# Three stages of a two-layer hybrid block trade places: hyena beside the second recurrent phase, attention after it, output weights where hyena was

## Chip, cores and metric

One core of one Trainium2 chip. The metric is device time in microseconds (us) of one execution; lower is better. The engines are named as in the profile: PE (TensorE matmul), PEld (its weight load), DVE (VectorE), ACT (ScalarE), POOL (GpSimd), SP (SyncE, which issues most of the transfers).

## The reference, cut to what matters

Two layers. In each, a normalised stream goes through one input projection, four mixers work on their parts of it, and an output projection adds the gated result to the stream. 1024 latent tokens, 256 context tokens, width 1024; each mixer has width 256.

```python
h_l = rms_norm(x, norm_g) * (1.0 + scale[:, None]) + shift[:, None]
hy_l, hyg_l, rw_l, rwg_l, wa_l, wag_l, fa_l, fag_l = jnp.split(h_l @ w_in, SPLIT_IDX, axis=-1)
a_l = hyena_branch(hy_l, ...) * jax.nn.silu(hyg_l)       # long convolution by FFT
b_l, b_c = rwkv_mixer(rw_c, rw_l, ...)                   # recurrent, both directions
c_l = window_attention(...) * jax.nn.silu(wag_l)         # +-128 tokens, and the context
d_l = dense_attention(...) * jax.nn.silu(fag_l)          # all 1280 tokens
mix_l = jnp.concatenate([a_l, b_l, c_l, d_l], axis=-1)
x = x + gate[:, None] * (mix_l @ w_out)
```

The context tokens pass through the same weights in the first layer and are not put out by the second. `scale`, `shift` and `gate` come from a modulation, silu(c) times a 1024 x 3072 matrix for each layer.

## The kernel before

The program is one straight stream of instructions, traced stage by stage (`program`, from L1573). A scheduler orders the instructions of each engine ahead of time, by the order in which they are traced and by a timing model of its own; at run time each engine, and each transfer queue, works its list in order. A tile waits by semaphores for earlier users of its addresses.

Tiles come from pools. A pool lies on the left or on the right side of SBUF: left pools are stacked upwards from 18.6 KB (per partition), right pools downwards from 224 KB; a closed pool's place is free for later pools of its side, and pools of opposite sides may overlap when they are open at different times. In both layers of the kernel before the stages lie as follows.

- Left: the projection's operands `hhi`, `hlo` (18.6 to 98.6 KB), above them the projection's own pool `pj` (to 137.7, with two buffers each of `wr`, `wh`, `wl`), above it the attention projection's pool `pa` (137.7 to 203.5). When operands and projection are done, attention's pool `at` takes 18.6 to 98.
- Right: hyena's filters first; in layer 0 then two modulations `mod` (209.8 to 224, three buffers of `mw`), one for the gate of this layer and one for the next layer; then phase A of the recurrence with its constants (204 to 224) and work tiles (138 to 204); then phase B (138.5 to 224); then hyena (102 to 224; `F` at 102 to 110); after it the output projection's weights and work tiles (99.9 to 224).

The stages: `Proj.rw` projects the seven recurrent blocks, with a convolution. `Proj.attn` (L295) projects queries, keys and values. `Rwkv.phase_a` (L444) prepares ten blocks of 128 tokens and after the 4th, 8th and 10th runs `solve`, 31 short steps on DVE and POOL. `Rwkv.phase_b` (L659) takes the ten blocks from both ends: `stage_b` loads `IN`, `yc`, `nn`, multiplies small blocks on PE, and `chain` carries the state; blocks that come too early for one direction are stored in `st_d` and taken up by `pend` at the end, seven of them after the tenth block. `hyena` (L1360) transforms, multiplies with `Kf` (two buffers) and transforms back, mostly on DVE and POOL. `attention` (L919) runs for a = 0, the windowed part, and a = 1, the dense part, in blocks of 128 queries: scores (L981), softmax, transposes, values; `om` at L1028 ends a block. `OutProj` (L1070) loads and splits the output weights (`wor`), then `tiles` works 128 tokens at a time; in the first layer it also writes the next layer's `hhi`, `hlo`, over attention's pool, and holds an `xt` tile (two buffers) until then.

The projection's other 14 blocks (three gates, six hyena blocks, one more gate) are `Proj.beside` (L283). Two of them go early (`PACE['pre']`); the rest is traced after phase B and is filler. It is paced by marks: each block of phase A sets a mark of weight 1.3, each of phase B one of 1.0 (the first 4.5), each of the last seven `pend` calls 0.5, 30 in all. A piece of projection may not be queued on PE ahead of the mark that its share falls to, between the fractions `f0` and `f1` of all marks.

Of the kernel before, what the change touches and what calls it, by code (L numbers as in the profile page):

```python
# [12 lines left out]
PSUM = bass.MemoryType.PSUM  # L13
# [10 lines left out]
PACE = {'pre': (2, 2), 'w0': (0.0, 0.0), 'wt': (3.5, 3.5), 'f0': (0.3, 0.3), 'f1': (0.7, 0.7)}  # L24
# [1335 lines left out]
def hyena(k, l, kd, sp, pp):  # L1360
# [27 lines left out]
    def forward(o_, hf):  # L1388
        u = U[hf]
        Kf = tile_([R, 2, 128], "Kf", 2, p)  # L1390
# [179 lines left out]
_OUT = (L, D)  # L1570


def program(nc, tc, A, out):  # L1573
# [3 lines left out]
    R = "right"  # L1577
    with k.pool("cp", 1) as cp, k.pool("dp", 1, DRAM) as dp:
        setup(k, cp, dp)

        def filters(l):
            for nm, f, _, shape in hyenas[:2 if l < DEPTH - 1 else 1]:
                k.kd[l, nm] = dp.tile(shape, F32, name=f"kd{l}{nm}")
                with tc.using_default_side(R), k.pool(f"hf{l}{nm}") as sp, k.pool(f"hfp{l}{nm}", 1, PSUM) as pp:
                    run(f(k, l, k.kd[l, nm], sp, pp))

        k.kd = {}
        for l in range(DEPTH):
            last = l == DEPTH - 1
            rw = Rwkv(k, l, cp, dp)  # L1590
            with ExitStack() as es:
                if l == 0:
                    held = ExitStack()
                    with tc.using_default_side(R):
                        ap = es.enter_context(k.pool("raw"))
                    hi, lo = norm_in(k, held.enter_context(k.pool(f"hp{l}")), ap)
                filters(l)
            with held:
                with k.pool(f"pj{l}") as sp, k.pool(f"pjp{l}", 1, PSUM) as pp:
                    w = Proj(k, l, hi, lo, sp, pp)  # L1600
                    run(w.rw())
                    todo = [(g, i) for g in (1, 2, 3, "h", 0) for i in range(6 if g == "h" else 2)]
                    early = PACE["pre"][l]
                    w.beside(todo[:early])
                    if not last:
                        for a, parts in ((l, (1,)), (l + 1, (0, 1))):
                            with tc.using_default_side(R), k.pool(f"mod{a}") as rs, k.pool(f"modp{a}", 1, PSUM) as rp:
# [3 lines left out]
                    with tc.using_default_side(R), k.pool(f"re{l}") as re, k.pool(f"ra{l}") as rs, k.pool(f"rap{l}", 1, PSUM) as rp:  # L1611
                        run(rw.phase_a(re, rs, rp))
                    with tc.using_default_side(R), k.pool(f"rb{l}") as rs, k.pool(f"rbp{l}", 1, PSUM) as rp:
                        run(rw.phase_b(rs, rp))
                    w.beside(todo[early:], PACE["f0"][l], PACE["f1"][l])
# [45 lines left out]
```

## Time and profile before

| | |
|---|---|
| median of 3 runs | 2611.66 us (2608.37 to 2614.43) |
| the profiled execution, its own time | 2599.59 us |
| span from its first to its last instruction | 2597.8 us |
| PE busy | 2294.4 us (88%) |
| DVE / ACT / POOL busy | 1696.6 / 1105.8 / 1012.8 us |
| mean granted TensorE clock | 0.913 of full |

Busy time is the time in which an engine had an instruction running; PE's is longer where the clock is at its lower level. The stages of layer 0, in us from the span's start: projection and filters to 264, attention projection and modulation to 434, phase A with its last solve to 722, phase B to 1040 (its seven late `pend` calls from 965), attention from 866 to 1278, hyena within that from 1040 to 1250, output projection to 1410. Layer 1: attention projection to 1719, phase A to 2010, phase B to 2292, hyena 2293 to 2461, attention 2119 to 2510, output projection to 2592.

### The profile page before, as it was taken

To read this page: it belongs to the slowest core of one execution; us is meant where nothing else is said; L and a number is where in the kernel's file an instruction comes from. 1 tells how busy PE (TensorE), PEld (TensorE's weight loads), DVE (VectorE), ACT (ScalarE), POOL (GpSimd) and SP (SyncE) were. 2 spreads that over 40 slices of the span, in tenths; PEclk is the share of its full clock that TensorE was granted. 3 is DMA by queue.
4 is the path that set the end of the run, shared out by engine and by line. 5 is a ranking of instruction groups with operands and counts; after the bars stand their busy time and mean duration, and the time that the engine had idled before them with its cause. 6 is when DMAs were issued, how large, how long until landed. Compare 5 with 4: busy or idle time off the path is not lost. (4 is left out here: it accounts for less than half of the span.)

```text
span 2597.8 us, 45285 instructions
## 1 busy us (share of the span) xinstructions
PE 2294.4 (88%) x16864; PEld 1873.1 (72%) x16864; DVE 1696.6 (65%) x3669; ACT 1105.8 (43%) x2622; POOL 1012.8 (39%) x1279
## 2 busy tenths in 40 slices
PE   7799999889999898878897997998999979887698
PEld 3688678667788786656686887976777868666466
DVE  6985247698734567797344776677886345779933
ACT  5422224444232576545444221344443347654451
POOL 1631223366622114464322233324676211336542
PEclk9899998779999899889998998987799989998799
DMA  7223773544364746411444124335445475641152
GB/s 261 93 90 112 247 219 116 151 143 147 107 228 141 196 150 159 165 33 70 139 129 133 72 74 152 114 112 147 136 133 161 161 201 171 163 154 49 42 162 98
DMA packets 288696, 359.12 MB, mean 138 GB/s; under 512 B 108007, under 2 KB 229910, under 8 KB 283100
## 3 DMA queue, kind: packets, MB, share of 16 engines
q1 hardware_dynamic: 264008, 271.04, 33.6%
q0 software_dynamic: 11232, 70.78, 7.9%
q10 hardware_dynamic: 13236, 14.40, 2.0%
q8 instruction: 133, 2.18, 0.3%
q14 instruction: 87, 0.71, 0.1%
HBM read 227.31 MB, written 128.84 MB: 137 GB/s over the span
## 5 line engine op out<-in xcount | busy, mean ns | idle before, releaser
L232 POOL TENSOR_TENSOR wl<-wr,wh 128x1024 fp32r<-128x1024 f32 x58 | 145.1, 2507 | 276.2 <-ACT wh L231 198.9
L986 DVE TENSOR_REDUCE st<-S 128x1 f32<-128x512 f32 (+1 forms) x320 | 173.2, 557 | 102.0 <-PE S L982 57.7
L245 PE MATMUL acc<-hhi,wh 128*128 128x512 f32 (+1 forms) x896 | 222.8, 387 | 15.0 <-ACT wh L231 10.0
L981 PE MATMUL S<-kp,qs 128*128 128x256 f32 (+2 forms) x384 | 151.0, 402 | 85.5 <-ACT P L996 64.1
L245 PE MATMUL acc<-hlo,wh 128*128 128x512 f32 (+1 forms) x896 | 215.8, 376 | 2.6 <-DVE hlo L211 2.6
L996 ACT ACTIVATE P<-S,st 128x512 f32<-128x512 f32 (+1 forms) x320 | 184.2, 588 | 79.4 <-DVE st L989 74.2
L245 PE MATMUL acc<-hhi,wl 128*128 128x512 f32 (+1 forms) x896 | 216.0, 376 | 0.0
L245 PEld LDWEIGHTS acc<-hhi,wh 128*128 128x128 f32 x896 | 160.8, 198 | 50.4 <-ACT wh L231 11.9
L1012 PE MATMUL pt<-ident,P 128*128 128x128 f32 x976 | 169.0, 296 | 29.8 <-ACT PT L952 23.3
L245 PEld LDWEIGHTS acc<-hlo,wh 128*128 128x128 f32 x896 | 157.8, 193 | 33.5 <-DVE hlo L211 3.1
L952 ACT COPY PT<-pt 128x512 f32<-128x512 f32 (+2 forms) x298 | 141.0, 497 | 88.0 <-PE pt L1012 86.2
L245 PEld LDWEIGHTS acc<-hhi,wl 128*128 128x128 f32 x896 | 155.1, 191 | 31.7 <-issue 3.2
L1012 PEld LDWEIGHTS pt<-ident,P 128*128 128x128 f32 x976 | 122.1, 150 | 61.6 <-ACT PT L952 30.7
L981 PEld LDWEIGHTS S<-kp,qs 128*128 128x128 f32 x384 | 78.5, 205 | 114.9 <-ACT P L996 78.0
L1022 PE MATMUL O<-PT,V 128*64 128x256 f32 x976 | 132.1, 388 | 3.3 <-ACT PT L952 2.7
L982 PE MATMUL S<-kp,qs 128*128 128x256 f32 (+2 forms) x384 | 126.7, 342 | 3.7 <-DMA kp<-qk_d 3.7
L1022 PEld LDWEIGHTS O<-PT,V 128*64 128x64 f32 x976 | 70.6, 138 | 45.6 <-issue 6.7
L340 ACT ACTIVATE qx<-acc 128x256 f32<-128x256 f32 x76 | 29.2, 385 | 171.6 <-PE acc L335 152.5
L231 ACT ACTIVATE wh<-wr 128x1024 fp32r<-128x1024 f32 x58 | 60.7, 1057 | 94.3 <-PE acc L245 75.0
L589 PEld LDWEIGHTS p_g<-AR,BKT 64*128 64x128 f32 x640 | 77.0, 221 | 30.9 <-issue 6.8
L335 PE MATMUL acc<-wh,hhi 128*128 128x256 f32 x608 | 95.0, 298 | 4.5 <-ACT qx L340 2.5
L335 PE MATMUL acc<-wl,hhi 128*128 128x256 f32 x608 | 92.4, 290 | 6.4 <-POOL wl L232 6.4
(404 smaller groups left out, 5918.7 us busy)
## 6 DMA issues: line engine op xcount, KB each, us to landing
IN<-in_d POOLq DMA_DIRECT2D x18, 2048.0 KB, 9.4
wr<-in_w_in POOLq DMA_DIRECT2D x58, 512.0 KB, 4.6
mw<-in_mod_w SPq DMA_DIRECT2D x48, 512.0 KB
in_d<-BK SPq DMA_DIRECT2D x20, 512.0 KB
in_d<-AL SPq DMA_DIRECT2D x20, 512.0 KB
kp<-qk_d SPq DMA_DIRECT2D x32, 320.0 KB
qk_d<-qo SPq DMA_DIRECT2D x72, 128.0 KB
in_d<-GG SPq DMA_DIRECT2D x18, 512.0 KB
```

The lines of the kernel that those rows point to most:

```text
L231: w.k.nc.scalar.activation(h, r, AF.Copy)
L232: w.k.nc.gpsimd.tensor_tensor(lw, r, h.bitcast(F32), op=ALU.subtract)
L245: nc.tensor.matmul(ps[:, :n], a[:, kc * 128:(kc + 1) * 128], b[:, kc, t0:t0 + n], start=(i == 0 and kc == 0), stop=(i == 2 and kc == 7))
L335: nc.tensor.matmul(ps[:, :256], x_[:, kc, t * 128:(t + 1) * 128], w_[:, kc, :], start=(n == 0 and kc == 0), stop=(n == 2 and kc == 7))
L589: nc.tensor.matmul(pg[:, hp, c], BKT[q, hp, c], AR[q, :, hp, half(c)], start=True, stop=True)
L952: nc.any.tensor_copy(o, i)
L981: nc.tensor.matmul(ps[:, w0:w0 + w], qs[:, hd % 2, hd // 2], kp[kv][0][:, t0:t0 + w], start=True, stop=False)
L982: nc.tensor.matmul(ps[:, w0:w0 + w], qs[:, hd % 2, hd // 2], kp[kv][1][:, t0:t0 + w], start=False, stop=not masks)
L986: TR(ng[:, i:i + 1], ps[:, :w0], axis=AX.X, op=ALU.max, negate=True)
L996: nc.scalar.activation(P[:, :w], ps[:, :w], AF.Exp, bias=gm, accum_out=den[:, i:i + 1])
L1012: nc.tensor.transpose(pt[:, i, :], P[:, i * 128:(i + 1) * 128], k.ident)
L1022: nc.tensor.matmul(O[kv * 64:kv * 64 + 64, 0], V[:, t, kv * 64:kv * 64 + 64], PTs[kv][:, i], start=(i == 0), stop=(i == nt - 1))
```

## The change

The side of every pool is given by `near` and `far` of the layer: near is left in layer 0 and right in layer 1, far is the other. Operands, projection, hyena and output weights lie near; filters, modulations, the attention projection, phases A and B, then attention, lie far. Hyena's `Kf` has one buffer instead of two, so that its pool has 114 KB and in layer 0 lies at 18.6 to 132.6 KB, clear of phase B. In layer 0 the attention projection's pool then lies at 158 to 224 KB, attention's at 144 to 224 and the output projection's at 18.6 to 142.6; layer 1 is the mirror image. The second half of `program` keeps its order of tracing. `PACE` releases the projection's pieces from the fraction 0.0 to 0.5 of the marks instead of 0.3 to 0.7.

```diff
-PACE = {'pre': (2, 2), 'w0': (0.0, 0.0), 'wt': (3.5, 3.5), 'f0': (0.3, 0.3), 'f1': (0.7, 0.7)}
+PACE = {'pre': (2, 2), 'w0': (0.0, 0.0), 'wt': (3.5, 3.5), 'f0': (0.0, 0.0), 'f1': (0.5, 0.5)}
...
-        Kf = tile_([R, 2, 128], "Kf", 2, p)
+        Kf = tile_([R, 2, 128], "Kf", 1, p)
...
+SIDES = ("left", "right")
...
+            near, far = SIDES[l % 2], SIDES[1 - l % 2]
+            on = tc.using_default_side
...
-                filters(l)
-            with held:
-                with k.pool(f"pj{l}") as sp, k.pool(f"pjp{l}", 1, PSUM) as pp:
...
+                filters(l, far)
+            with held, on(near), k.pool(f"pj{l}") as sp, k.pool(f"pjp{l}", 1, PSUM) as pp:
...
+                with on(far):
                     if not last:
                         for a, parts in ((l, (1,)), (l + 1, (0, 1))):
-                            with tc.using_default_side(R), k.pool(f"mod{a}") as rs, k.pool(f"modp{a}", 1, PSUM) as rp:
+                            with k.pool(f"mod{a}") as rs, k.pool(f"modp{a}", 1, PSUM) as rp:
                                 modulation(k, a, parts, 3, rs, rp)
                     with k.pool(f"pa{l}") as sa, k.pool(f"pap{l}", 1, PSUM) as pq:
                         run(w.attn(sa, pq))
-                    with tc.using_default_side(R), k.pool(f"re{l}") as re, k.pool(f"ra{l}") as rs, k.pool(f"rap{l}", 1, PSUM) as rp:
+                    with k.pool(f"re{l}") as re, k.pool(f"ra{l}") as rs, k.pool(f"rap{l}", 1, PSUM) as rp:
                         run(rw.phase_a(re, rs, rp))
...
             with ExitStack() as es:
+                with on(near):
+                    for nm, _, f, _ in hyenas[:1 if last else 2]:
+                        with k.pool(f"hy{l}{nm}") as rs, k.pool(f"hyp{l}{nm}", 1, PSUM) as rp:
+                            run(f(k, l, k.kd[l, nm], rs, rp))
                 at = ExitStack()
-                for nm, _, f, _ in hyenas[:1 if last else 2]:
-                    with tc.using_default_side(R), k.pool(f"hy{l}{nm}") as rs, k.pool(f"hyp{l}{nm}", 1, PSUM) as rp:
-                        run(f(k, l, k.kd[l, nm], rs, rp))
-                sp, pp = at.enter_context(k.pool(f"at{l}")), at.enter_context(k.pool(f"atp{l}", 1, PSUM))
-                with tc.using_default_side(R):
+                with on(far):
+                    sp, pp = at.enter_context(k.pool(f"at{l}")), at.enter_context(k.pool(f"atp{l}", 1, PSUM))
+                with on(near):
                     op = OutProj(k, l, es.enter_context(k.pool(f"op{l}")), es.enter_context(k.pool(f"opp{l}", 1, PSUM)))
...
-                    hi, lo = operands(held.enter_context(k.pool(f"hp{l + 1}")))
...
+                    with on(far):
+                        hi, lo = operands(held.enter_context(k.pool(f"hp{l + 1}")))
```

## Rows read from the trace of the kernel before

**Rows 1.** The page: engine busy (share) xinstructions; a costliest group (busy, mean ns).
```profile
PE 2294.4 (88%) x16864; PEld 1873.1 (72%) x16864; DVE 1696.6 (65%) x3669; ACT 1105.8 (43%) x2622; POOL 1012.8 (39%) x1279
...
L986 DVE TENSOR_REDUCE st<-S 128x1 f32<-128x512 f32 (+1 forms) x320 | 173.2, 557 | 102.0 <-PE S L982 57.7
```

**Rows 2.** Busy time by stretch, layer 0; columns in the first line.
```profile
core 0: us, PE busy (x) PEld busy (x) DVE busy (x) ACT busy (x) POOL busy (x), PEclk, DMA share, GB/s
264.60:366.50 101.90, 99.49 (x654) 68.86 (x655) 27.57 (x123) 21.98 (x50) 19.16 (x13) 0.98 0.74 242
434.00:722.00 288.00, 258.83 (x1596) 206.94 (x1593) 225.57 (x425) 122.45 (x243) 159.40 (x280) 0.84 0.48 144
722.00:965.00 243.00, 227.85 (x2794) 199.78 (x2795) 117.36 (x355) 112.95 (x325) 51.12 (x93) 0.96 0.56 176
965.00:1040.00 75.00, 65.09 (x651) 48.41 (x650) 59.81 (x239) 52.55 (x170) 28.33 (x37) 0.95 0.57 147
1052.00:1215.00 163.00, 123.64 (x798) 99.21 (x798) 144.90 (x227) 79.50 (x215) 95.57 (x71) 0.85 0.21 71
1278.00:1410.00 132.00, 117.94 (x542) 97.42 (x542) 50.73 (x69) 59.64 (x130) 39.47 (x40) 0.93 0.35 113
```

**Rows 3.** The same view of layer 1: phase B, its end, the output projection.
```profile
2010.00:2219.00 209.00, 189.90 (x2429) 167.01 (x2429) 98.54 (x304) 107.06 (x314) 36.66 (x69) 0.96 0.57 179
2219.00:2292.00 73.00, 62.77 (x643) 44.96 (x640) 56.31 (x211) 49.08 (x146) 26.81 (x35) 1.00 0.49 131
...
2510.00:2592.00 82.00, 76.50 (x338) 63.01 (x336) 34.63 (x39) 15.58 (x22) 26.20 (x25) 0.98 0.33 112
```

**Rows 4.** Timeline of SP: start us, us, engine line op; phase B's last store, hyena.
```profile
1039.75 0.36 SPq L848 DMA_DIRECT2D mix_d<-om  x1
1040.41 0.35 SPq L1368 DMA_DIRECT2D F<-in_fw  x1
```

**Rows 5.** Timeline of all engines: the modulation's last store, phase A's first constant.
```profile
366.50 0.32 SPq L140 DMA_DIRECT2D mrow<-mr  x1
...
368.34 0.33 ACTq L456 DMA_DIRECT2D tri<-in_tri  x1
```

**Rows 6.** The modulation's loads, one line: ns min/median/max, first to last start.
```profile
L126 SPq DMA_DIRECT2D mw<-in_mod_w x29: 328/345/904, 265.7 to 358.0; - x29
```

**Rows 7.** Busy time of the modulation's matmuls (L129): PE, PEld, PEclk, DMA, GB/s.
```profile
264.60:366.50 101.90, 32.19 (x128) 3.35 (x128) 0.98 0.74 242
```

**Rows 8.** The same for the projection pieces' matmuls (L245) in phase B.
```profile
722.00:838.00 116.00, 73.20 (x345) 56.68 (x345) 1.00 0.49 166
```

**Rows 9.** One line: phase A's block stores; phase B's first matmuls, layers 0 and 1.
```profile
L621 SPq DMA_DIRECT2D in_d<-AL x10: 332/394/472, 459.4 to 671.7; - x10
...
L733 PE MATMUL p_t<-IN,Y x160: 270/275/484, 722.3 to 951.2; 128*128 128x128 f32 x160
...
L733 PE MATMUL p_t<-IN,Y x160: 270/275/553, 2009.6 to 2205.8; 128*128 128x128 f32 x160
```

**Rows 10.** Key tile `kp` in 700 to 900 us: first scores, key loads.
```profile
L981 PEld LDWEIGHTS S<-kp,qs x24: 186/190/331, 866.4 to 898.5; 128*128 128x128 f32 x24
...
L933 SPq DMA_DIRECT2D kp<-qk_d x8: 444/594/1663, 836.6 to 843.6; - x8
```

**Rows 11.** Timeline of POOL, layer 1: ends of two windowed, two dense blocks.
```profile
2245.00 0.73 POOL L1028 TENSOR_TENSOR om<-om,gt 128x256 f32<-128x256 f32 x1 [0.80 <-ACT om L1027]
2256.12 0.73 POOL L1028 TENSOR_TENSOR om<-om,gt 128x256 f32<-128x256 f32 x1
2283.13 0.74 POOL L1028 TENSOR_TENSOR om<-om,gt 128x256 f32<-128x256 f32 x1 [4.07 <-ACT om L1027]
2303.70 0.73 POOL L1028 TENSOR_TENSOR om<-om,gt 128x256 f32<-128x256 f32 x1 [12.77 <-ACT om L1027]
```

**Rows 12.** Line L1234 in hyena of layer 1: ns min/median/max.
```profile
L1234 DVE TENSOR_TENSOR W<-G x4: 1104/1534/2185, 2323.8 to 2434.8; 128x512 f32<-128x512 f32 x4
L1234 DVE TENSOR_TENSOR Z<-G x4: 675/886/1095, 2351.7 to 2453.5; 128x512 f32<-128x512 f32 x4
```

**Rows 13.** SP's waits, 2295 to 2462 us: waited for, us in total, times, longest.
```profile
SPq L1451 <- DVE zc L1447: 54.1, 1, 54.1
```

More of the change, by code (lines that the diff above doesn't have):

```diff
@@ L1576, in program, with filters @@
     run = lambda g: [None for _ in g]
-    R = "right"
     with k.pool("cp", 1) as cp, k.pool("dp", 1, DRAM) as dp:
         setup(k, cp, dp)
-        def filters(l):
+        def filters(l, side):
             for nm, f, _, shape in hyenas[:2 if l < DEPTH - 1 else 1]:
                 k.kd[l, nm] = dp.tile(shape, F32, name=f"kd{l}{nm}")
-                with tc.using_default_side(R), k.pool(f"hf{l}{nm}") as sp, k.pool(f"hfp{l}{nm}", 1, PSUM) as pp:
+                with tc.using_default_side(side), k.pool(f"hf{l}{nm}") as sp, k.pool(f"hfp{l}{nm}", 1, PSUM) as pp:
                     run(f(k, l, k.kd[l, nm], sp, pp))
@@ L1589, in program @@
             last = l == DEPTH - 1
+            near, far = SIDES[l % 2], SIDES[1 - l % 2]
+            on = tc.using_default_side
             rw = Rwkv(k, l, cp, dp)
-            with ExitStack() as es:
+            with ExitStack() as es, on(far):
                 if l == 0:
                     held = ExitStack()
-                    with tc.using_default_side(R):
-                        ap = es.enter_context(k.pool("raw"))
-                    hi, lo = norm_in(k, held.enter_context(k.pool(f"hp{l}")), ap)
-                filters(l)
-            with held:
-                with k.pool(f"pj{l}") as sp, k.pool(f"pjp{l}", 1, PSUM) as pp:
[L1600 to L1604, printed above, removed]
+                    ap = es.enter_context(k.pool("raw"))
+                    with on(near):
+                        hp = held.enter_context(k.pool(f"hp{l}"))
+                        hi, lo = norm_in(k, hp, ap)
+                filters(l, far)
+            with held, on(near), k.pool(f"pj{l}") as sp, k.pool(f"pjp{l}", 1, PSUM) as pp:
+                w = Proj(k, l, hi, lo, sp, pp)
+                run(w.rw())
+                todo = [(g, i) for g in (1, 2, 3, "h", 0) for i in range(6 if g == "h" else 2)]
+                early = PACE["pre"][l]
+                w.beside(todo[:early])
+                with on(far):
                     if not last:
                         for a, parts in ((l, (1,)), (l + 1, (0, 1))):
-                            with tc.using_default_side(R), k.pool(f"mod{a}") as rs, k.pool(f"modp{a}", 1, PSUM) as rp:
+                            with k.pool(f"mod{a}") as rs, k.pool(f"modp{a}", 1, PSUM) as rp:
                                 modulation(k, a, parts, 3, rs, rp)
@@ L1631, in program @@
                     held = ExitStack()
-                    hi, lo = operands(held.enter_context(k.pool(f"hp{l + 1}")))
-                    with k.pool(f"nrmp{l}", 1, PSUM) as pp:
-                        op.tiles([8, 9] + list(range(8)), out, (hi, lo, pp))
+                    with on(far):
+                        hi, lo = operands(held.enter_context(k.pool(f"hp{l + 1}")))
+                        with k.pool(f"nrmp{l}", 1, PSUM) as pp:
+                            op.tiles([8, 9] + list(range(8)), out, (hi, lo, pp))
 def arrays_of(inputs):
```

6 lines of the change are left out of this document (3 added, 3 removed).

## The prediction

> **What bounds the kernel now.** I read the page's engine line first, then the busy time by stage, then the gates between stages. TensorE (PE) is busy for 2294.4 of 2597.8 us [rows 1], so the time can only fall where PE idles or is granted its lower clock level. The stage views [rows 2, 3] show where that is. Phase A of the recurrence has a mean clock of 0.84, which is a mix of the two levels. Phase B is well filled in both layers (0.96), by projection pieces first and by attention later. The worst stretch is hyena beside attention: PE is busy for 123.6 of 163 us at clock 0.85, while VectorE (DVE) is busy for 144.9. So attention with phase B is a good pairing, attention with hyena a bad one, and phase A lacks filler in its first half. The change moves all three. I follow the time at which phase B starts, phase B's length, what is left after it, and the last projection.
>
> **Gates.** The sum hangs on one reading of the kernel: when a pool is placed on addresses of an older pool, its first instructions are queued behind the last of the older one. In this kernel hyena's first table F lies at 102 to 110 KB and phase B's pool only begins at 138.5 KB, but hyena's pool as a whole covers both. F is loaded right behind phase B's last store, at 1040.41 after 1039.75 [rows 4]. Likewise phase A's constant `tri`, at 206 KB, comes behind the modulation's last store, at 368.34 after 366.50 [rows 5], though the modulation lies above 209 KB. So I ask, for each pool, whom it overlaps after the change.
>
> **Part by part, first layer.** Phase B's start moves as follows.
> (1) The attention projection's pool goes to the far side, top-aligned at 158 to 224 KB. It now lies over the two modulations, which hold their place until their last load is used. Today both run together from 264.6 to 366.5. The modulation's 29 loads of 0.524 MB are 15.2 MB, 63 us at the 242 GB/s of that stretch [rows 2, 6]; I take 52, since alone they don't share the DMA engines. Its own matmuls keep PE busy for 32.2 us [rows 7]. Today modulation and attention projection end together at 434, 169 us after 264.6; then it would be 52 + (169 - 32) = 189, so +20 (0 if they still overlap, +31 at 63 us). Filler for that gap is unlikely: the loads of the attention projection's own weights take both `wr` buffers and wait.
> (2) Phase A's constants lie under the same pool and can't come early any more. From hyena's first load (1040.41) to the stretch that starts with its first transposes (1052) are 12 us [rows 2, 4]; the first pieces of the later projections have no mark to wait for and cover some: +8 (0 to 12).
> (3) The projection pieces. Marks weigh 13 for phase A, 13.5 for phase B's blocks, 3.5 for its end, 30 in all. Pieces were released between marks 9 and 21, now between 0 and 15, so 87% by the end of phase A's blocks. 73.2 us of them ran after 722 [rows 8] and move ahead. Phase A with its solves has 288 - 258.8 = 29 us of idle PE, and 16% of 288 = 46 us lost to the clock [rows 2], 75 in all, so they just fit: +6 (0 to 25). The last solve stays: between phase A's last block (671.7) and phase B's first matmul (722.3) are 51 us [rows 9]. Projection covers it today; then it is the pieces that are left and hyena's start, and what idles there costs no more than the 51 us already on the path.
> Together phase B starts 34 us later.
> (4) Phase B with hyena. B's ten blocks and its end take 722 to 1040, 318 us, and in layer 1 2010 to 2292, 282 us [rows 2, 3]; block starts are (951.2 - 722.3)/9 = 25.4 us apart in layer 0 and 21.8 in layer 1 [rows 9], with PE full. With hyena PE has room, but DVE hasn't: phase B's stretches hold 117 + 60 us and hyena's 145, less attention's share, of which the reductions alone are 173.2/2 = 87 a layer [rows 1, 2]. That leaves at most 235 us of DVE work. Taken at 19 us a block, 48 for the end (75 and 73 today with attention in it) and 22 for waits on SP (below), I get 260 and 256: -58 and -26. Lower end 225, at about the DVE work; upper end 300.
> (5) Attention now lies on the phase's side, 144 to 224 KB, and starts only at phase B's end. From its first key load to its first score matmul are 866.4 - 836.6 = 30 us today [rows 10], beside phase B's own loads; I take 22, bare. A block of the windowed part takes 11.1 us without hyena, one of the dense part 20.6 [rows 11]. First layer: ten blocks, two short, 108; dense 8 x 20.6 + 2 x 7.5 = 180. With the weights there early, output tiles of the context and the first latent tile slip into its gaps for another 3. That is 22 + 108 + 183 = 313 from phase B's end to attention's end, against 1278 - 1040 = 238: +75.
> (6) Output projection. Its weights load beside attention instead of behind hyena. In the first layer its pace is held by two `xt` buffers until attention's pool is free, so about 3 of 10 tiles go ahead: 132 [rows 2] becomes 92, -40.
> Layer 0: 34 - 58 + 75 - 40 = +11.
> **Second layer.** No modulation, so (2) + (3) = +14. Phase B -26. After its end: today 2292 to 2592, 300 us. Then 22 + 8 x 11.3 + 8 x 20.6 = 277, plus what of the output's 76.5 PE us [rows 3] does not fit into dense attention's gaps (PE is busy for 62.8 of 73 us in phase B's end, so 14% of 165 = 23 us): 54, and 3 for the last tile's end, 334 in all, +34. Layer 1: +22.
> Kf with one buffer costs nothing by itself: its load can start when the last product is done, a whole transform before its use; it lies on SP's queue, and that is the next point.
> **Sum:** 2599.6 (the profiled execution) + 33 = 2633. The median of the three runs, 2611.7, stands 12 us above that execution, so 2645.
>
> **A rule weighed.** DVE's sum `W` from `G` in hyena's forward takes 1104 to 2185 ns, the same sum into `Z` 675 to 1095 [rows 12], and POOL is busier around the first. The Trainium skill, "SBUF — State Buffer", "Who interferes with whom", says that a DVE instruction with two SBUF inputs and a GpSimd one that reads SBUF hold the shared port against each other, and that one with a single SBUF input is free of it. The trace agrees as far as the spread of `W` goes. By that rule phase B's own POOL work, 51 + 28 us [rows 2], now stands against hyena's DVE sums, and up to 79 us more a layer would be blocked; the sum above leaves it out.
>
> **Rivals.**
> Faster: hyena fits into phase B. PE has idle slots there, DVE's work of 235 us is less than the 318 that phase B takes now, and most of B's DVE steps read PSUM. If both phases close in 225 us, the sum is 33 - 35 - 31 = -33: 2579. It decides at about 240 to 245 us.
> Slower, by SP's queue. In layer 1, hyena's store waits on SP for 54.1 us at one place [rows 13], since transfers were queued for times that the engines don't keep. Today only attention's query loads stand behind; then it is phase B's `yc`, `nn` and `st_d` transfers, and its one ST buffer waits for its store. With one Kf buffer there are three such waits a layer. Phase B of 300 us each: +33 + 40 + 44 = 2729.
> The pools don't hold as I read them: modulation stays hidden (-20), and attention starts inside phase B's end (-22 and about -25, twice): 33 - 114 = -81, 2531. Against it: both gates [rows 4, 5].
>
> **How the numbers follow.** Chances: forecast (slower, about 2617 to 2690) 0.44; SP's queue 0.15; hyena fits 0.28; pools 0.05; a sum that ends near nothing 0.08. The predicted time is the first case's, 2645. The range goes to the faster case with some of its spread and to the slow one, 2570 to 2722; outside are the pool rival and the tails. What counts as no change is 0.2%, 5 us, about what a measurement can tell. Faster 0.33, same 0.08, slower 0.59.
>
> **What would show it.** In the profile after: `rope` loads behind the modulation's last store (1); phase A's `tri` behind the attention projection (2); phase B's first matmul 30 to 40 us later in layer 0 and 14 in layer 1, relative to the layer's start (3); block starts 18 to 22 us apart and `kp` not before phase B's last store (4, 5); in layer 1 output matmuls between dense attention blocks (6). It is wrong if phase B with hyena closes in under 240 us, if dense blocks alone run faster than 20 us, or if the stretch from 264 to phase A does not grow.

## The result, and the profile after

The changed kernel takes 2796.73 us (median; 2792.12 to 2808.99), the kernel before 2610.01 us in the same measurement: ratio 1.073, interval 1.0681 to 1.0778. It is slower, as forecast, but by 187 us where the sum had 33, and outside the range.

The page of the profile after, engine busy (share):

```profile
PE 2299.3 (82%) x16864; PEld 1867.0 (67%) x16864; DVE 1734.7 (62%) x3707; ACT 1097.7 (39%) x2584; POOL 1019.9 (37%) x1279
```

Against [rows 1], PE has the same number of instructions and is busy for 5 us more, in a span 196 us longer (2794.0 against 2597.8). So no matmul work was added; PE stands idle for 191 us more. Busy time by stretch shows where (columns as in [rows 2]). First layer: modulation alone; attention projection; phase A's blocks; its end up to phase B's first matmul; phase B with hyena; the gap before attention; what is left of the output projection.

```profile
264.00:337.00 73.00, 42.75 (x138) 5.11 (x136) 1.95 (x8) 5.95 (x8) 8.03 (x5) 0.79 0.73 249
337.00:472.00 135.00, 134.96 (x1083) 133.00 (x1082) 80.97 (x316) 40.93 (x109) 42.54 (x35) 0.99 0.37 109
483.00:748.00 265.00, 253.47 (x1688) 202.84 (x1689) 208.24 (x362) 126.76 (x246) 153.40 (x231) 0.95 0.50 150
748.00:813.00 65.00, 43.58 (x242) 37.57 (x242) 30.77 (x79) 14.39 (x25) 28.90 (x73) 0.84 0.60 220
813.00:1094.00 281.00, 196.28 (x2653) 177.54 (x2651) 212.91 (x399) 61.38 (x155) 154.62 (x166) 0.79 0.43 145
1094.00:1121.00 27.00, 5.54 (x9) 2.34 (x10) 1.01 (x9) 6.61 (x8) 9.31 (x4) 0.63 1.00 261
...
1448.00:1530.00 82.00, 62.13 (x296) 51.27 (x296) 35.31 (x50) 49.32 (x117) 30.23 (x31) 0.89 0.37 132
```

The same view of the second layer: phase B with hyena, the gap, windowed attention, dense attention with output tiles, the end.

```profile
2169.00:2415.00 246.00, 165.15 (x2392) 149.47 (x2392) 180.30 (x349) 58.30 (x148) 124.64 (x143) 0.78 0.42 141
2415.00:2443.00 28.00, 4.17 (x6) 1.60 (x7) 0.71 (x8) 5.42 (x6) 9.32 (x4) 0.56 1.00 270
2443.00:2538.00 95.00, 81.48 (x583) 61.94 (x583) 51.36 (x205) 77.03 (x248) 14.53 (x11) 0.93 0.39 106
2538.00:2748.00 210.00, 193.94 (x1139) 143.27 (x1137) 101.88 (x246) 115.47 (x310) 24.59 (x26) 0.98 0.19 60
2748.00:2794.00 46.00, 24.96 (x96) 20.04 (x96) 8.52 (x11) 4.74 (x7) 6.94 (x7) 0.78 0.19 63
```

Phase B shows the exchange. Before, its PE was busy for 292.9 of 318 us at clock 0.96 to 0.95 [rows 2]; now for 196 of 281 us at 0.79. The stage became shorter by 37 us and leaves PE idle for 85 us. The gates that the prediction named stand where it put them. SP's timeline has `rope`, the attention projection's first load, right behind the modulation's last store, and hyena's first loads ahead of phase B's `yc`:

```profile
338.62 0.33 SPq L140 DMA_DIRECT2D mrow<-mr  x1
338.99 0.42 SPq L300 DMA_DIRECT2D rope<-in_rope  x1
...
781.41 0.32 SPq L276 DMA_DIRECT2D gt_d<-gt  x1
781.83 0.38 SPq L1368 DMA_DIRECT2D F<-in_fw  x1
782.25 1.53 SPq L1374 DMA_DIRECT2D zc<-hy_d  x2
...
784.51 0.49 SPq L710 DMA_DIRECT2D yc<-ys_d  x1
```

Phase A's `tri` on ACT's queue, behind the attention projection, and phase A's first matmul on PE:

```profile
469.23 0.33 ACTq L456 DMA_DIRECT2D tri<-in_tri  x1
...
483.47 2.07 PE L486 MATMUL p_w<-wup,LW 65*128 65x512 f32 x2 [5.86 <-DMA LW<-rw_d]
```

Phase B's first matmuls (line L733 of layers 0 and 1; first to last start) answer to [rows 9]:

```profile
L733 PE MATMUL p_t<-IN,Y x160: 275/275/552, 812.9 to 1022.8; 128*128 128x128 f32 x160
...
L733 PE MATMUL p_t<-IN,Y x160: 274/311/580, 2168.8 to 2354.5; 128*128 128x128 f32 x160
```

Phase B starts at 812.9 instead of 722.3, and with it 91 us of the first layer's loss are already there. In the second layer it starts 637 us after the first layer's last operand is written, instead of 599. The sum against the two traces, change in us:

| step | layer 0 forecast | measured | layer 1 forecast | measured |
|---|---|---|---|---|
| (1) to (3): phase B's start | +34 | +91 | +14 | +38 |
| (4): phase B with hyena | -58 | -37 | -26 | -36 |
| (5), (6): from phase B's end to the layer's end | +35 | +67 | +34 | +73 |
| layer | +11 | +121 | +22 | +75 |

### The profile page after: what moved, and what is told of

It reads as the page before. It is cut to its first block, busy times and chain, and to the rows that moved or that the text cites. A ratio compares the mean times of both kernels' runs of the same rounds, so it can differ in the third digit from the quotient of the medians.

```text
span 2794.0 us, 45325 instructions
## 1 busy us (share of the span) xinstructions
PE 2299.3 (82%) x16864; PEld 1867.0 (67%) x16864; DVE 1734.7 (62%) x3707; ACT 1097.7 (39%) x2584; POOL 1019.9 (37%) x1279
## 5 line engine op out<-in xcount | busy, mean ns | idle before, releaser
L245 PE MATMUL acc<-hhi,wh 128*128 128x512 f32 (+1 forms) x896 | 225.3, 387 | 13.0 <-ACT wh L231 9.1
L245 PE MATMUL acc<-hhi,wl 128*128 128x512 f32 (+1 forms) x896 | 225.6, 382 | 0.0
L245 PE MATMUL acc<-hlo,wh 128*128 128x512 f32 (+1 forms) x896 | 221.4, 380 | 2.9 <-DVE hlo L211 2.9
L245 PEld LDWEIGHTS acc<-hhi,wh 128*128 128x128 f32 x896 | 159.4, 198 | 47.6 <-ACT wh L231 11.1
L981 PE MATMUL S<-kp,qs 128*128 128x256 f32 (+2 forms) x384 | 142.8, 380 | 56.3 <-ACT P L996 22.0
L245 PEld LDWEIGHTS acc<-hlo,wh 128*128 128x128 f32 x896 | 157.9, 194 | 35.7 <-issue 5.4
L245 PEld LDWEIGHTS acc<-hhi,wl 128*128 128x128 f32 x896 | 156.8, 193 | 34.4 <-issue 8.1
L1028 POOL TENSOR_TENSOR om<-om,gt 128x256 f32<-128x256 f32 x36 | 26.4, 733 | 411.1 <-ACT om L1027 411.1
L1012 PE MATMUL pt<-ident,P 128*128 128x128 f32 x976 | 160.0, 286 | 19.6 <-ACT PT L952 10.6
L1012 PEld LDWEIGHTS pt<-ident,P 128*128 128x128 f32 x976 | 112.2, 143 | 59.3 <-ACT PT L952 20.0
L952 ACT COPY PT<-pt 128x512 f32<-128x512 f32 (+2 forms) x245 | 113.9, 497 | 62.4 <-PE pt L1012 61.9
L982 PE MATMUL S<-kp,qs 128*128 128x256 f32 (+2 forms) x384 | 122.0, 331 | 2.8 <-DMA kp<-qk_d 2.8
L1123 POOL TENSOR_TENSOR y<-y,xt 128x512 f32<-128x512 f32 x36 | 49.6, 1382 | 173.1 <-DVE y L1122 80.7
L1121 PE MATMUL ops<-woh,mh 128*128 128x512 f32 x288 | 83.1, 432 | 21.2 <-ACT mh L1112 21.2
```

The costliest lines, as they stand in the source:

```text
L245: nc.tensor.matmul(ps[:, :n], a[:, kc * 128:(kc + 1) * 128], b[:, kc, t0:t0 + n], start=(i == 0 and kc == 0), stop=(i == 2 and kc == 7))
L952: nc.any.tensor_copy(o, i)
L981: nc.tensor.matmul(ps[:, w0:w0 + w], qs[:, hd % 2, hd // 2], kp[kv][0][:, t0:t0 + w], start=True, stop=False)
L982: nc.tensor.matmul(ps[:, w0:w0 + w], qs[:, hd % 2, hd // 2], kp[kv][1][:, t0:t0 + w], start=False, stop=not masks)
L1012: nc.tensor.transpose(pt[:, i, :], P[:, i * 128:(i + 1) * 128], k.ident)
L1121: nc.tensor.matmul(ps, a[:, kc, :], b[:, kc, s], start=(n == 0 and kc == 0), stop=(n == 2 and kc == 7))
```

## The experiments

Three questions: what delays phase B's start (place of the attention projection, pace of the pieces, hyena's loads), what hyena costs beside phase B and on which engine, and why attention with the output tiles takes longer than summed. All ratios are to the kernel before on the same chip; stretches and stages are read from one profiled execution of each kernel.

**The attention projection back on the near side.**

```diff
-                    with k.pool(f"pa{l}") as sa, ...
+                    with on(near), k.pool(f"pa{l}") as sa, ...
```

> The changed kernel with one thing put back: the attention projection's pool lies on the near side again, above the projection's pool, clear of the modulations and of phase A's constants. Theory (its place over the modulations is what makes it wait): its first matmul comes at about 271 us instead of 337, phase A's first matmul at about 433 instead of 483.5 in layer 0, and in layer 1 phase A starts some 17 us earlier; all later stages keep their lengths, so 2797 - 50 - 17 = about 2730 us. Rival (the modulation's loads cost the same time wherever they stand, the sum's +20): phase A starts at 455 to 465, and the whole is 2760 to 2780. Rival (what is saved ahead of phase A is lost behind it, since the projection pieces that filled phase A then run out earlier): under 20 us, 2780 or more.

Measured: 2763.18 us, ratio 1.0621 (1.0591 to 1.0651). The stretch in which the modulation had stood alone:

```profile
264.00:337.00 73.00, 70.00 (x449) 48.10 (x449) 20.32 (x80) 15.11 (x32) 17.88 (x12) 0.98 0.79 266
```

PE is full again: the place was what made it wait. Phase A's first matmul comes at 447 instead of 483.5, 36 us, and the whole gains 34 by the medians, 28 by the ratios. The total lies in the second theory's range, but phase A starts earlier than that theory has it. It is not the 50 of the first theory: 434 [rows 2] isn't reached, and 447 comes back below in a kernel whose projection never moved, so those 13 us belong to the pace. In layer 1 phase A starts 9 us earlier after the layer's start, but phase B doesn't (639 us after it, against 637 in the changed kernel): the saving is lost again by phase B's start, as the third theory had it, and the place costs nothing there.

**The pace of before in the changed kernel.**

```diff
-PACE = {..., 'f0': (0.0, 0.0), 'f1': (0.5, 0.5)}
+PACE = {..., 'f0': (0.3, 0.3), 'f1': (0.7, 0.7)}
```

> The changed kernel with the projection pieces released between 0.3 and 0.7 of the marks, as before. Theory (phase A is lengthened by the pieces it was given, and phase B with hyena has PE to spare): phase A goes from 265 back to about 240 us in layer 0, phase B with hyena grows by less than that; 10 to 30 us faster in all. Rival (hyena needs its projected rows): with pieces still running in phase B hyena starts 60 to 100 us later and its end falls behind phase B's end, attention and the output weights wait for nothing but the hyena rows come late; 20 to 60 us slower. Rival: phase A is bound by its own vector work and doesn't change.

Measured: 2835.06 us, ratio 1.0905 (1.0879 to 1.0931), 38 us slower than the changed kernel by the medians, 46 by the ratios. Phase B of layer 0:

```profile
768.00:1117.00 349.00, 260.86 (x3052) 230.33 (x3052) 220.88 (x418) 81.54 (x186) 166.31 (x188) 0.85 0.44 153
```

Phase A falls from 265 to 234 us and phase B starts 45 us earlier, at 768, but it takes 349 us instead of 281. Hyena's first load `F` comes at 887.1, just behind the last piece's store at 883.8: its pool lies on the place of the projection and its operands, so later pieces mean a later hyena, which then runs until 1121, past phase B's end. The second theory's outcome, by a place rather than by rows alone. In this arrangement the early pace is the better of the two that were run.

**The kernel before with the new pace alone.**

```diff
-PACE = {..., 'f0': (0.3, 0.3), 'f1': (0.7, 0.7)}
+PACE = {..., 'f0': (0.0, 0.0), 'f1': (0.5, 0.5)}
```

> The kernel before with only the new pace of the projection pieces (0.0 to 0.5 of the marks). It sizes step (3) by itself, in stages that are otherwise those of before. Theory (the pieces cost in phase A what they take on PE beyond its idle time, and phase B is shortened by the pieces it no longer holds): phase A is 15 to 25 us longer than its 239, phase B's first matmul comes 20 to 30 us later, phase B and attention in it end about as before or earlier since attention can start earlier in it: within 10 us of before. Rival (what the sum says, +6): phase B starts within 12 us of before and the whole is 15 to 40 us faster. Rival (phase B needs this filler): 10 to 40 us slower.

Measured: 2645.40 us, ratio 1.0145 (1.0112 to 1.0178). Phase A's blocks and what lies between them and phase B, layer 0:

```profile
447.00:712.00 265.00, 252.21 (x1723) 203.40 (x1723) 211.26 (x366) 128.38 (x247) 154.29 (x231) 0.97 0.51 152
712.00:787.00 75.00, 38.05 (x189) 31.49 (x188) 33.41 (x109) 14.23 (x40) 29.86 (x76) 0.75 0.65 178
```

Phase B starts 65 us later than in the kernel before (787), in layer 1 38 us later after the layer's start (637 against 599): in layer 1 all of what the changed kernel shows. In layer 0 it is made of 13 us of pieces queued ahead of phase A, 26 in its ten blocks (265 against 239), and 24 behind them, where the pieces have run out and PE is busy for only 38 of 75 us. What makes that last stretch longer isn't shown: attention's early loads and scores lie in it too (its first scores at 778), and in the kernel without hyena, below, it is 52 us with the pieces gone just as early. The kernel gets some of it back, since attention starts before phase B, but is 38 us slower in all: the third theory, at the upper end of its 10 to 40.

**Later paces in the kernel before.**

```diff
+PACE = {..., 'f0': (0.4, 0.4), 'f1': (0.8, 0.8)}
```

> The kernel before with the pieces released between 0.4 and 0.8 of the marks, later than its 0.3 to 0.7; 0.0 to 0.5 made it 38 us slower. Theory (a piece costs in phase A more than it costs in phase B, where it is ready filler): phase A 232 to 239 us, phase B starts up to 7 us earlier, but attention starts later in phase B: within 15 us of before. Rival (the effect is one slope): 10 to 20 us faster. Rival (attention, which needs the place of the projection, is what suffers): 15 to 40 us slower.

Measured: 2669.36 us, ratio 1.0261 (1.0229 to 1.0293). Phase A takes 219 us, phase B starts 3 us earlier, and attention 59 us later (first scores at 925). That is the third theory's way, but 66 us slower where it had 15 to 40. With 0.3 to 0.9:

```diff
+PACE = {..., 'f0': (0.3, 0.3), 'f1': (0.9, 0.9)}
```

> The kernel before with the pieces released between 0.3 and 0.9 of the marks: the same start, the last pieces late in phase B. Theory (phase B is full on PE anyway, and attention's place comes free only when the last piece is done): attention starts 60 us later or more, phase B's late part and the stretch behind it grow: 15 to 50 us slower. Rival (fewer pieces in phase A's last solve, same total): within 10 us.

Measured: 2695.14 us, ratio 1.0355 (1.0316 to 1.0394), 92 us slower, beyond the 50 at the upper end of its first theory; first scores at 978, attention's end some 110 us later. Of the four paces that were run in the kernel before, its own is the best. Phase A's length goes with the pieces that it holds: its ten blocks take 219, 239 and 265 us with 23, 64 and 149 us of the pieces' matmuls (L245) among them, for a start at 0.4, 0.3 and 0.0; with 0.3 to 0.9 it is 243 us with 63. So in these blocks a piece costs about a third of the time that it keeps PE busy.

**Phase B alone.** Hyena left out:

```diff
-                    for nm, _, f, _ in hyenas[:1 if last else 2]:
-                        with k.pool(f"hy{l}{nm}") as rs, ...:
-                            run(f(k, l, k.kd[l, nm], rs, rp))
+                    for hf in range(2):
+                        nc.sync.dma_start(out=k.mix_d[s, 0:n], in_=k.gt_d[s, 0:n])
```

> The changed kernel without hyena's transforms (its rows of the mix are copies of gate rows), so phase B runs alone, without filler. It measures phase B's own length. Theory (phase B is bound by its own chain of small steps, hyena costs little beside it): layer 0 still over 255 us of the 281, layer 1 over 225 of the 245. Rival (hyena's vector and POOL work stands in phase B's way): under 230 and 205. On the way to phase B: if hyena's first loads delay phase B's, the stretch from phase A's last store to phase B's first matmul falls from 65 us to 50. At its end: the output weights can then load during phase B; if they are what holds attention's keys back, the gap from phase B's last store to the first scores falls from 27 us to 12 to 16.

Measured: 2607.45 us, ratio 1.0027 (1.0005 to 1.0048). Without hyena's transforms the changed kernel takes as long as the kernel before with them. From phase A's last store to phase B's last store:

```profile
745.00:984.00 239.00, 166.28 (x2532) 147.41 (x2530) 126.42 (x360) 65.56 (x162) 81.55 (x167) 0.83 0.52 173
2000.00:2225.00 225.00, 147.65 (x2258) 130.89 (x2256) 117.37 (x339) 58.79 (x149) 68.73 (x156) 0.81 0.51 168
```

and in the changed kernel:

```profile
748.00:1094.00 346.00, 239.86 (x2893) 215.10 (x2892) 243.68 (x477) 75.77 (x180) 183.52 (x238) 0.80 0.46 159
2110.00:2415.00 305.00, 192.03 (x2541) 173.37 (x2539) 228.78 (x441) 67.11 (x164) 161.68 (x222) 0.78 0.47 159
```

Phase B alone takes 187 us in layer 0 (797 to 984) and 183 in layer 1 (2042 to 2225), a block 13 to 14 us, its end 54. The first theory (over 255 us) falls: phase B isn't bound by its own chain of steps, hyena stretches it by 94 and 63. Counted from phase A's last store hyena costs 107 and 80, because phase B also starts later beside hyena: 65 and 59 us behind that store against 52 and 43. With hyena's loads in it, the DMA engines are full for the last 32 us of that stretch; these 32 us in the changed kernel, and the whole stretch without hyena:

```profile
781.00:813.00 32.00, 11.55 (x81) 11.02 (x82) 6.93 (x20) 6.96 (x14) 5.54 (x11) 0.68 0.99 369
...
745.00:797.00 52.00, 31.91 (x161) 26.54 (x160) 27.74 (x71) 8.22 (x14) 29.85 (x76) 0.85 0.51 182
```

The gap before attention stays at 26 and 28 us with no hyena in the way.

**Where hyena's cost comes from.** Three kernels took parts of it out. First, without the arithmetic between the transforms:

```diff
-        W = tile_(...); S, D = ...; ft.pair(...); ft.eight(W, ...); products with Kf; ft.eight(Z, ...)
+        for q, rs in enumerate(((1, 3), (5, 7), (0, 2), (4, 6))):
+            nc.scalar.activation(Z[:, 2 * q:2 * q + 2], tr(rs), AF.Copy)
```

> The changed kernel with hyena's arithmetic between its transforms left out (forward only evacuates its four products on ACT and hands them to the inverse): loads, stores, PE work and the order of SP's queue stay, about 100 us of DVE and 84 us of POOL work a layer go. Phase B alone was 187 and 183 us, with hyena 281 and 246. Theory (the arithmetic stands in DVE's list ahead of phase B's own short steps): phase B falls to what it is alone plus hyena's PE time, 215 to 230 in layer 0 (with the context's hyena) and 195 to 210 in layer 1. Rival (SP's queue: hyena's loads and stores stand ahead of phase B's): phase B stays at 260 and 230 or more. Rival (PE: the two have simply too much matmul work at the lower clock): 250 and 225.

Then with the POOL half put back (sums `AB1`, `even`, the products of rows 0 to 3, the sums `S`, all through `nc.gpsimd`):

> As the kernel without hyena's arithmetic, but with about the POOL half of it put back (sums, products with Kf and the back sums of half the rows, the same shapes; the DVE half stays out). Theory (DVE's list is what phase B waits in): phase B is within 12 us of the kernel without any arithmetic, in both layers. Rival (POOL: phase B's own POOL copies and its chain wait behind hyena's POOL steps, or DVE's copies are held by POOL): phase B is 25 us or more above that kernel, and DVE's share of the cost is the smaller one.

Then with the DVE half instead (`pair`, `TU`, `odd`, `AB`, the products of rows 4 to 7, the sums `D`, all through `nc.vector`):

> The counterpart of the run with the POOL half: hyena's DVE half stays as it is, its POOL half is left out (where a tile would be unwritten, ACT copies something into it). Counted from phase A's last store to phase B's last store, layers 0 and 1 so far: without hyena 239 and 226 us, without its arithmetic 285 and 247, with the POOL half 318 and 265, with both 346 and 305. Theory (each engine's in-order list delays phase B by itself, the parts add up): 313 and 287. Rival (DVE alone sets it, and POOL's half only counts because DVE steps wait for it): 335 or more and 298 or more. Rival (POOL sets it): under 298 and under 262.

Measured, in that order: 2688.16, 2736.13 and 2730.42 us. Without arithmetic phase B itself takes 203 and 182 us, below what the theory gave, but it starts later; so the stretches are again those from phase A's last store to phase B's last store. Without arithmetic:

```profile
752.00:1037.00 285.00, 214.32 (x2890) 192.05 (x2888) 140.90 (x385) 79.27 (x184) 91.77 (x174) 0.87 0.56 193
2053.00:2300.00 247.00, 181.59 (x2547) 164.15 (x2545) 123.10 (x351) 72.66 (x173) 73.49 (x158) 0.85 0.58 196
```

with the POOL half:

```profile
754.00:1072.00 318.00, 222.21 (x2890) 199.44 (x2888) 159.29 (x383) 82.87 (x189) 162.53 (x238) 0.82 0.49 173
2083.00:2348.00 265.00, 183.64 (x2545) 165.72 (x2544) 128.95 (x345) 76.25 (x178) 144.22 (x222) 0.82 0.54 183
```

with the DVE half:

```profile
752.00:1066.00 314.00, 225.74 (x2891) 202.57 (x2889) 205.21 (x480) 87.89 (x197) 96.33 (x174) 0.83 0.50 175
2078.00:2346.00 268.00, 189.53 (x2546) 169.96 (x2544) 187.29 (x441) 80.17 (x186) 81.72 (x158) 0.82 0.54 181
```

| us over phase B alone | layer 0 | layer 1 |
|---|---|---|
| loads, matmuls, evacuation, the inverse (in layer 0 also the context's hyena) | 46 | 22 |
| POOL half, on top | 33 | 18 |
| DVE half, on top | 29 | 21 |
| both, beyond the two together | -1 | 19 |
| sum | 107 | 80 |

So no single engine sets it. The theory that DVE's list alone holds phase B back falls (the POOL half costs as much), and so does the rival by which POOL alone does. In layer 0 the parts add up (314 us, the theory's 313); in layer 1 the DVE half gives 268 where the theory had 287, and some 19 us come only from both halves together. Each removal also lets the scheduler order the lists anew (without the arithmetic it put 29 us of hyena's matmuls ahead of phase B's first block), so single figures may be off by several us.

What one such delay looks like, in DVE's timeline of the changed kernel, layer 1 (start us, us, engine, line, instruction):

```profile
2241.47 1.21 DVE L1231 SCALAR_TENSOR_TENSOR G<-s,s 128x512 f32<-128x512 f32 x1
2242.71 1.10 DVE L1234 TENSOR_TENSOR W<-G 128x512 f32<-128x512 f32 x1
2243.74 1.21 DVE L1235 TENSOR_TENSOR W<-G 128x512 f32<-128x512 f32 x1
2244.98 1.30 DVE L1409 TENSOR_TENSOR t<-W,Kf 128x1024 f32<-128x1024 f32 x1
2246.20 1.27 DVE L742 TENSOR_TENSOR Z<-p_w,IN 128x512 f32<-128x512 f32 x2
```

and on PE in the same stretch:

```profile
2241.73 1.95 PE L740 MATMUL p_w<-T,NO 128*128 128x128 f32 x16
...
2246.93 2.05 PE L747 MATMUL p_q<-Z,Y 128*128 128x128 f32 x16 [3.25 <-DVE Z L742]
```

Phase B's `p_w` is done at 2243.7, but its `Z` starts at 2246.20, behind two of hyena's steps that stand ahead of it in DVE's list, and PE waits 3.25 us. That is the theory's picture; the runs show that it is a part of the cost, not the whole.

SP's queue, the rival that was to make phase B slow, isn't what does it: with all of hyena's loads and stores left in and only the arithmetic gone, phase B itself takes 203 and 182 us, where that rival had 260 and 230 or more. SP's two longest waits on hyena, 781 to 1094 us (us in total, times, longest):

```profile
SPq L1561 <- DVE S L804: 12.9, 1, 12.9
...
SPq L1451 <- DVE zc L1447: 4.2, 2, 3.6
```

The first is the context's store; hyena's own stores hold SP for 4.2 us, against 54.1 in [rows 13]. With the smaller ones SP waits on hyena for 21 us in layer 0 and 25 in layer 1, about the 22 that the sum of (4) allowed.

**Copies held by POOL.**

```diff
-                cpy(y[p:p + 32, :, p:p + 32], yc[p:p + 32])
+                nc.scalar.activation(y[p:p + 32, :, p:p + 32], yc[p:p + 32], AF.Copy)
```

> The changed kernel with phase B's copies from yc to Y all on ACT. On DVE they take 0.29 us alone, but up to 4.03 us where POOL is working for hyena at the time. Theory (a DVE copy is held until POOL's instruction ends, and what is queued behind it on DVE with it): 5 to 15 us faster than 2797. Rival (the hold is hidden, or ACT's list is no better place): within 5 us or slower.

Measured: 2800.13 us, ratio 1.0751 (1.0721 to 1.0781), not distinguishable from the changed kernel's 1.073: the rival. The hold is real in the trace (last section), but it is worth little or hidden, and on ACT the copy takes 0.41 us.

**The output weights traced behind attention.**

```diff
-                with on(near):
-                    op = OutProj(k, l, ...)
                 for a in range(2):
                     run(attention(k, l, a, sp, pp))
+                with on(near):
+                    op = OutProj(k, l, ...)
```

> The changed kernel with the output projection's pool and weights traced behind attention instead of ahead of it. Theory (the output tiles among the dense blocks cost their own PE time and the sum's free gaps are not there): dense blocks fall from 28 to 30 us to about 20.6, attention ends some 20 us (layer 0) and 50 us (layer 1) earlier, and the output projection behind it grows by as much: within 15 us of the changed kernel. Rival (the filler breaks the order of attention and costs more than it brings): 20 to 60 us faster. Rival (what the sum says: tiles slip in nearly free): 30 us or more slower. The gap ahead of the first scores falls below 20 us in both if the weights' loads are what holds the keys back.

Measured: 2795.68 us, ratio 1.0745 (1.0718 to 1.0771): no change. The gap before the first scores falls from 27 and 28 us to 19 in both layers, so 8 us of it were the weights' loads, which SP issues ahead of the keys. The whole doesn't gain by it. On the dense blocks the run says nothing, since the scheduler put the tiles among them again, with 28 to 30 us a block. So another kernel held them back by force.

**Output tiles held until attention's last matmul.**

```diff
+                k.mark(1.0)
+                op.hold = k.marks[-1][1]
...
-                        nc.tensor.matmul(ps, a[:, kc, :], b[:, kc, s], ...)
+                        with k.behind(w.hold):
+                            nc.tensor.matmul(ps, a[:, kc, :], b[:, kc, s], ...)
```

> The changed kernel with the output projection's matmuls held on PE until attention's last one; weights, loads and splits stay where they are. Theory (PE is nearly full in the dense blocks, and a tile among them costs what it saves behind them): dense blocks fall to 20 to 21 us, attention ends some 20 us earlier in layer 0 and 40 to 50 in layer 1, what is behind it grows by as much, and the whole stays within 12 us of 2797. Rival (the sum's: a dense block has 3 to 4 us of free PE, the tiles use it): 25 to 45 us slower. Rival (tiles in front of the scores break attention's order): 25 us or more faster.

Measured: 2789.85 us, ratio 1.0695 (1.0662 to 1.0729), 7 us less than the changed kernel at the median, which the two intervals don't tell apart. Dense attention and the output projection, layers 0 and 1:

```profile
1254.00:1399.00 145.00, 127.12 (x814) 84.25 (x815) 73.20 (x199) 98.18 (x283) 5.10 (x7) 0.99 0.11 30
1399.00:1528.00 129.00, 118.61 (x559) 98.70 (x557) 51.46 (x69) 57.54 (x128) 33.40 (x37) 0.97 0.34 110
2533.00:2688.00 155.00, 134.57 (x852) 89.20 (x851) 78.70 (x215) 103.08 (x295) 6.29 (x9) 0.99 0.13 37
2688.00:2780.00 92.00, 86.33 (x381) 71.16 (x379) 35.31 (x39) 15.58 (x22) 25.33 (x25) 0.98 0.29 100
```

A dense block is 19.1 us without tiles. In layer 1 dense attention shrinks from 210 us to 155, and what is behind it grows from 46 to 92: 55 given, 46 taken. In layer 0 the eight long dense blocks shrink from 204 us to 152, and what is behind them grows from 82 to 129. The tiles beside attention were worth nothing, as the first theory had it.

No kernel that computes the whole came out faster than the kernel before. The best of the changed kind is the one with the attention projection on the near side, at 1.0621.

## Why the prediction was right in sign and wrong in size

**What bounds the kernel, and the pairings: right.** PE's busy time is what it was, and the loss is idle PE. Attention is good company for phase B because it brings matmuls. But the prediction didn't follow this to its end. It held hyena beside phase B for a saving of 84 us in both layers, and attention alone for a cost of 75 us in layer 0 and, with the output, 34 in layer 1. Phase B alone takes 187 and 183 us: beside it hyena costs 107 and 80, so it isn't hidden there. The company of before was the better one: 318 us, 131 more than alone, paid for 73 us of pieces [rows 8], ten windowed blocks and the two short dense ones; these twelve take 122 us by themselves after the change (1121 to 1243).

**(1), (2), the gates: right, sizes short.** Modulation alone took 74 us from 264.6 to its last store at 338.62, not 52. The step "alone they don't share the DMA engines" failed. The 29 loads did go out in 62 us (266.8 to 329.1) instead of 92 [rows 6], but the whole stretch moved 249 GB/s, hardly more than both streams together before, 242 [rows 2]. The DMA engines' share was 0.73, so they weren't full; SP waited for 32 us, 26 times, for a `mw` buffer that a matmul still held, and a load took 5.1 us to land. From the last load to the last store lie another 9.5 us. The sum's upper bound of 63 us was the nearer value. With (2), the place cost 36 us, against 28. In layer 1 it cost nothing.

**(3), the pieces: the step that failed most.** +6 with a bound of 25 in layer 0, where the traces show about 55 (91 less the 36 of the place), and 38 in layer 1. Three parts make up the 55: 13 us of pieces queued ahead of phase A, 26 in its ten blocks, 13 of hyena's loads ahead of phase B. The room in phase A was counted as 29 us of idle PE and 46 us of low clock, 75 in all, into which the pieces "just fit". The clock did rise, from a mean of 0.81 in the blocks (434 to 672) to 0.95, but the pieces don't fit in for nothing: they cost about a third of their PE time there. In 459 to 588 us of the kernel before, at clock 0.71, the blocks came every 21.5 us with PE busy for 107 and DVE for 106 of 129 us; with the pieces they come 25.4 us apart (511 to 638), with PE busy for 122 of 127 us at 0.97, 74 of them pieces. So the higher clock didn't shorten a block; what a block waits for without pieces isn't shown. And "what idles there costs no more than the 51 us already on the path" was right of the last solve itself, 52 us without hyena though PE is then busy for only 32 of them, but beside hyena the stretch is 65 and 59 us against 52 and 43. The sum had nothing for hyena's loads ahead of phase B's.

**(4), phase B with hyena: nearly right, by luck.** 260 and 256 forecast, 281 and 246 measured: in the two layers together 11 us short. It lies between the rivals, not near the point of 240 to 245 at which hyena would fit in layer 0, and just at it in layer 1. The reason given, one DVE total of 235 us, is not what the runs show: DVE was busy for 213 of 281, and the POOL half costs as much as the DVE half. The total came near because the estimates happened to add up, not by the mechanism. Block starts are 23 and 20 us apart (18 to 22 forecast), and phase B's end, which nothing fills, takes 58 and 55 us at clock 0.65 and 0.57 instead of 48.

**(5), (6), attention and output: the second failing.** Gap 22 forecast, 27 and 28 measured: here [rows 10] was the better value, and "bare" was wrong, since 8 us are the output weights' loads that SP issues ahead of the keys. The windowed part came out as summed, 110 us in layer 0 (the tenth `om` on POOL at 1230.65) against 108, and the two short dense blocks took 13 (15 summed). The step that failed is the dense part with its tiles: its eight long blocks take 204 us in layer 0 (1243.4 to 1447.9) and 210 in layer 1, where the sum had 165, with 3 more for the tiles in layer 0 and none in layer 1. It took a block as 20.6 us with output tiles in free PE slots, about 3 of 10 tiles in layer 0 and 23 us of PE work in layer 1; the scheduler put 70 and 77 us of tile matmuls there. A dense block alone takes 19.1 us and leaves 12% of PE idle, but the tiles hardly used it: with them a block takes 24 to 31. In layer 0 it is 409 us from the first scores to the layer's end (1121 to 1530), against 400 with the tiles behind (1128 to 1528). The 40 us of (6) were earned (50, from 132 to 82) and spent again in (5).

**Rivals.** "The pools don't hold as I read them" falls on every gate. "SP's queue" falls by the kernel without the arithmetic and by SP's waits. "Hyena fits" falls in layer 0 and is at its border in layer 1, while the loss lies elsewhere. The range's upper end of 2722 came from the case of a slow phase B; that phase B's start and the work behind its end are short at once, by 57 and 32 us in layer 0 and 24 and 39 in layer 1, wasn't among the cases.

## What to carry to other kernels

Before two stages are paired, ask for each what it takes alone and what the pair takes together: here phase B alone was 187 us and 281 beside hyena, and it started later too, while attention fills a phase that leaves PE free. Filler has a price in its new place: phase A's blocks paid about a third of its PE time, though PE had idle time and a low clock there. The first loads of a stage that moves ahead belong into the sum (13 and 16 us here). Filler for an engine that was already 88% busy bought nothing. And a stage at low clock isn't therefore bound by the clock: phase A's blocks became longer, not shorter, with the filler that raised it.

## What the runs showed of the hardware

One thing that hadn't been expected: short DVE copies in phase B, with one SBUF input, were held until POOL's work in hand was over. The copies from `yc` in the changed kernel (ns min/median/max), POOL's timeline around the longest, and the same copies with only the POOL half and with only the DVE half of hyena's arithmetic:

```profile
L665 DVE COPY Y<-yc x39: 275/290/4027, 804.8 to 2342.5; 32x256 f32<-32x256 f32 x39
...
2251.86 2.34 POOL L1410 TENSOR_TENSOR W<-W,Kf 128x1024 f32<-128x1024 f32 x1
2254.16 1.25 POOL L1418 TENSOR_TENSOR s<-W 128x512 f32<-128x512 f32 x1
...
L665 DVE COPY Y<-yc x40: 271/288/10530, 810.3 to 2275.7; 32x256 f32<-32x256 f32 x40
...
L665 DVE COPY Y<-yc x39: 263/284/436, 808.2 to 2276.9; 32x256 f32<-32x256 f32 x39
```

The copy that starts at 2251.54 ends with POOL's second step, 4.03 us later. With the POOL half alone one takes 10.53 us, through ten POOL steps that follow each other; with the DVE half alone none takes over 0.44 us, without hyena 0.28 to 0.50. So it is POOL's work that holds them. DVE's copies from PSUM (`Q` from `p_q`) take 0.43 us at most in all of these runs. In the changed kernel ten of DVE's copies from SBUF (`Y`, `NO`) take over 0.6 us, 11 us in both layers beyond their usual time, so little was to be gained on ACT.

The prediction took instructions with a single SBUF input for free of POOL, without a condition, and weighed hyena's two-input sums instead. The Trainium skill, "SBUF — State Buffer", section "Who interferes with whom", frees them only outside the two-port modes, and says that a copy which runs in a two-port mode and a GpSimd instruction hold the shared ports against each other; the rows agree, though none shows the mode in which a copy ran.

The 79 us a layer that the prediction named for the sums didn't come: hyena's DVE steps in layer 1 sum to 115 us beside phase B and 116 beside attention, phase B's to 108 with hyena and 102 without. But the sums do wait for POOL, in both kernels alike, for hyena's own POOL half. With that half left out the 106 DVE steps of layer 1 sum to 81 us, and hyena's POOL steps sum to 77 us without the DVE half and 89 with it. One of the lines, in layer 1 of the changed kernel and with the DVE half alone (before: [rows 12]):

```profile
L1234 DVE TENSOR_TENSOR W<-G x4: 676/1098/2597, 2153.7 to 2283.5; 128x512 f32<-128x512 f32 x4
...
L1234 DVE TENSOR_TENSOR W<-G x4: 679/686/700, 2121.3 to 2196.7; 128x512 f32<-128x512 f32 x4
```

How much of hyena's cost beside phase B goes through this isn't shown.
